# Rotary embedding: whole batches with 32 KB rows, and loads and stores in one in-order queue

## The chip, the cores and the metric

One core of one Trainium2 chip. The metric is the device time in microseconds (us), as a median of several executions. Each kernel was also executed once under the profiler. A profile's span is about 1.8 us shorter than the time of the same execution.

## The reference

```python
# x: 8 batches x 2048 positions x 8 heads x 64, float32; cos, sin: 2048 x 32
x1, x2 = x[..., :32], x[..., 32:]
out1 = x1 * cos - x2 * sin
out2 = x1 * sin + x2 * cos
out = concatenate([out1, out2], axis=-1)
```

x and the output are 33.55 MB each, the tables 0.26 MB each. Every byte is read or written once.

## The kernel before

A partition holds 16 consecutive positions, so a batch is 128 rows of 32 KB. The kernel cuts each batch into two slabs of 2 MB with rows of 16 KB. Loads are issued on the sync queue, stores on the scalar queue, and nine slab buffers lie between them.

```python
    SL = 8                      # positions of a slab, of 16 in a partition
    SLAB = SL * HD              # 4096 floats, 16 KB
    UNIT = 4 * HD
    NBUF = 9
...
    nc.scalar.dma_start(out=cos_sb, in_=cos_src)
    for i in range(NBUF):
        load(i)                 # nc.sync.dma_start, slab 0 in four pieces
...
    kinds = {}
    for i in (5, 10):
        kinds |= {(i, 0): "C", (i, UNIT): "B"}
```

A usual piece of 128x2048 (kind A) is two products of 128x1024 on GpSimd and one product and one addition on VectorE. Kind B leaves the addition to TensorE (two products with the identity matrix, summed in PSUM) and the copy out of PSUM to ScalarE. Kind C takes GpSimd out as well: VectorE makes both products, TensorE sums.

```python
        keep(nc.vector.tensor_mul(out=t1..., in0=xk, in1=rep(cos_ps[...], 2 * H)))
        if kind == "A":
            keep(nc.vector.tensor_add(out=xt, in0=t1, in1=t2))
...
    for i in range(last + 1):
        if i == last:
            for k in range(i - LAG, i):
                store(k, 0, SLAB)          # nc.scalar.dma_start
        for lo, n in spans(pieces(i)):
            rotate(i, lo, n)
            if i == last:
                store(i, lo, n)
        if LAG <= i < last:
            store(i - LAG, 0, SLAB)
        if i > LAG and i - LAG - 1 + NBUF <= last:
            load(i - LAG - 1 + NBUF)
```

Of the kernel before, what the change touches and what calls it, by code (L numbers as in the profile page):

```python
# [9 lines left out]
@with_exitstack  # L10
def kernel(
    ctx: ExitStack,
    tc: tile.TileContext,
    x: bass.AP,
    cos: bass.AP,
    sin: bass.AP,
    out: bass.AP,
):
    nc = tc.nc
    keep = tc.keep_in_program_order  # L20
    f32 = mybir.dt.float32
    PSUM = bass.MemoryType.PSUM

    B, S, H, D = x.shape
    Dh = D // 2
    P = 128
    HD = H * D
    R = S // P

    SL = 8  # L30
    n_half = R // SL
    SLAB = SL * HD
    UNIT = 4 * HD
    NBUF = 9
    C = 512

    xv = x.rearrange("b (q r) h d -> b q (r h d)", q=P)
    ov = out.rearrange("b (q r) h d -> b q (r h d)", q=P)
    cos_src = cos.rearrange("(q r) d -> q r d", q=P)
    sin_src = sin.rearrange("(q r) d -> q r d", q=P)  # L40

    const_pool = ctx.enter_context(tc.tile_pool(name="const", bufs=1))
    tab_pool = ctx.enter_context(tc.tile_pool(name="tab", bufs=1, space=PSUM))
    t1_pool = ctx.enter_context(tc.tile_pool(name="t1p", bufs=1, space=PSUM))
    o_pool = ctx.enter_context(tc.tile_pool(name="op", bufs=2, space=PSUM))
    t1s_pool = ctx.enter_context(tc.tile_pool(name="t1s", bufs=3))
    xpool = ctx.enter_context(tc.tile_pool(name="xpool", bufs=NBUF))
    t2_pool = ctx.enter_context(tc.tile_pool(name="t2p", bufs=3))

    cos_sb = const_pool.tile([P, R, Dh], f32, tag="cb")  # L50
    sin_sb = const_pool.tile([P, R, Dh], f32, tag="sb")
    nsin = const_pool.tile([P, R, Dh], f32, tag="ns")
    eye = const_pool.tile([P, P], f32, tag="eye")
    neye = const_pool.tile([P, P], f32, tag="neye")
    cos_ps = tab_pool.tile([P, R, Dh], f32, tag="cp")
    sin_ps = tab_pool.tile([P, R, Dh], f32, tag="sp")

    slabs = [(b, l) for l in range(n_half) for b in range(B)]
    last = len(slabs) - 1
    xts = {}  # L60

    def cuts(i):
        if i == 0:
            return [HD, HD, 2 * HD, UNIT]
        return [SLAB]

    def pieces(i):
        if i == 0:
            return [HD, HD, 2 * HD, UNIT]
        if i == last:  # L70
            return [UNIT, 2 * HD, HD, HD]
        return [UNIT, UNIT]

    def spans(sizes):
        lo = 0
        for n in sizes:
            yield lo, n
            lo += n

    def load(i):  # L80
        b, l = slabs[i]
        xt = xpool.tile([P, SLAB], f32, tag="xt", name=f"xt{i}")
        for lo, n in spans(cuts(i)):
            nc.sync.dma_start(
                out=xt[:, lo : lo + n],
                in_=xv[b, :, l * SLAB + lo : l * SLAB + lo + n],
            )
            if i == 0 and lo == 0:
                nc.sync.dma_start(out=sin_sb, in_=sin_src)
        xts[i] = xt  # L90

    nc.scalar.dma_start(out=cos_sb, in_=cos_src)
    for i in range(NBUF):
        load(i)

    nc.gpsimd.memset(eye, 0.0)  # L96
    nc.gpsimd.affine_select(
        out=eye,
        in_=eye,
        compare_op=mybir.AluOpType.not_equal,  # L100
        fill=1.0,
        base=0,
        pattern=[[-1, P]],
        channel_multiplier=1,
    )
    nc.scalar.mul(nsin, sin_sb, -1.0)  # L106
    nc.scalar.mul(neye, eye, -1.0)
    nc.vector.tensor_copy(cos_ps, cos_sb)  # L108
    nc.scalar.copy(sin_ps, sin_sb)  # L109

    def rep(a, n):
        return dataclasses.replace(a, ap=[a.ap[0][:], a.ap[1][:], [0, n], a.ap[-1][:]])

    kinds = {}
    for i in (5, 10):
        kinds |= {(i, 0): "C", (i, UNIT): "B"}

    def rotate(i, lo, n):
        b, l = slabs[i]
        kind = kinds.get((i, lo), "A")  # L120
        xt = xts[i][:, lo : lo + n]
        r0 = l * SL + lo // HD
        nr = n // HD
        xk = xt.rearrange("p (r k d) -> p r k d", r=nr, d=Dh)
        xu = xt.rearrange("p (g u d) -> p g u d", u=2, d=Dh)
        if kind == "A":
            t1 = t1_pool.tile([P, n], f32, tag="t1")
        else:
            t1 = t1s_pool.tile([P, n], f32, tag="t1s")
        if kind == "C":  # L130
            t2 = t1s_pool.tile([P, n], f32, tag="t1s")
        else:
            t2 = t2_pool.tile([P, n], f32, tag="t2")
        t1u = t1.rearrange("p (g u d) -> p g u d", u=2, d=Dh)
        t2u = t2.rearrange("p (g u d) -> p g u d", u=2, d=Dh)
        if kind != "C":
            for u, tab in ((1, sin_sb), (0, nsin)):
                nc.gpsimd.tensor_mul(  # L138
                    out=t2u[:, :, u, :].rearrange("p (r h) d -> p r h d", h=H),
                    in0=xu[:, :, 1 - u, :].rearrange("p (r h) d -> p r h d", h=H),  # L140
                    in1=rep(tab[:, r0 : r0 + nr, :], H),
                )
        keep(
            nc.vector.tensor_mul(  # L144
                out=t1.rearrange("p (r k d) -> p r k d", r=nr, d=Dh),
                in0=xk,
                in1=rep(cos_ps[:, r0 : r0 + nr, :], 2 * H),
            )
        )
        if kind == "A":  # L150
            keep(nc.vector.tensor_add(out=xt, in0=t1, in1=t2))  # L151
        elif kind == "B":
            for j in range(n // C):
                o = o_pool.tile([P, C], f32, tag="o")
                cs = slice(j * C, (j + 1) * C)
                nc.tensor.matmul(o, eye, t1[:, cs], start=True, stop=False)  # L156
                nc.tensor.matmul(o, eye, t2[:, cs], start=False, stop=True)  # L157
                keep(nc.scalar.copy(xt[:, cs], o))  # L158
        else:
            keep(  # L160
                nc.vector.tensor_mul(  # L161
                    out=t2.rearrange("p (r k d) -> p r k d", r=nr, d=Dh),
                    in0=xk,
                    in1=rep(sin_ps[:, r0 : r0 + nr, :], 2 * H),
                )
            )
            G = C // Dh
            for u in range(2):
                for j in range(n // 2 // C):
                    o = o_pool.tile([P, C], f32, tag="o")  # L170
                    gs = slice(j * G, (j + 1) * G)
                    nc.tensor.matmul(o, eye, t1u[:, gs, u, :], start=True, stop=False)  # L172
                    nc.tensor.matmul(  # L173
                        o, eye if u else neye, t2u[:, gs, 1 - u, :], start=False, stop=True
                    )
                    keep(nc.scalar.copy(xu[:, gs, u, :], o.rearrange("p (g d) -> p g d", d=Dh)))  # L176

    LAG = 2

    def store(i, lo, n):  # L180
        b, l = slabs[i]
        keep(
            nc.scalar.dma_start(
                out=ov[b, :, l * SLAB + lo : l * SLAB + lo + n],
                in_=xts[i][:, lo : lo + n],
            )
        )

    for i in range(last + 1):
        if i == last:  # L190
            for k in range(i - LAG, i):
                store(k, 0, SLAB)
        for lo, n in spans(pieces(i)):
            rotate(i, lo, n)
            if i == last:
                store(i, lo, n)
        if LAG <= i < last:
            store(i - LAG, 0, SLAB)
        if i > LAG and i - LAG - 1 + NBUF <= last:
            load(i - LAG - 1 + NBUF)  # L200


# [28 lines left out]
```

## Time and profile before

| | before |
|---|---|
| time, median of 3 (later 6) runs | 164.75 (164.68) us |
| span of the profiled run | 163.0 us |
| bytes moved | 67.66 MB, mean 415 GB/s |
| share of 16 DMA engines' span in use | 98.2% |
| VectorE, GpSimd busy | 88%, 86% |
| packet of 16 KB on one DMA engine | 611 ns |

Read the DMA share first.

### The profile page before, as it was taken

The page shows a single profiled execution, that of the slowest core. Times are in us where ns is not written, and L with a number is a line of the kernel's source. Part 1 is how long each engine was busy: PE and PEld are TensorE (multiplying, and loading weights), DVE is VectorE, ACT ScalarE, POOL GpSimd, SP SyncE. Part 2 cuts the span into 40 slices and gives each one's busy share as a digit, 9 for nine tenths or more (in the row PEclk, how much of TensorE's full clock was granted, in tenths as well). Part 3 has the DMA queues.
Part 4 walks back from the last instruction along what each step waited for, and adds up shares of the span by engine and source line. Part 5 has one row for each costly group of instructions (what it writes and reads, how often), then busy time and mean ns, then how long its engine had stood idle before and what let it go on. Part 6 is the DMA issues. An engine that isn't in the chain of part 4 may idle for free. (4 is left out here: it accounts for less than half of the span.)

```text
span 163.0 us, 480 instructions
## 1 busy us (share of the span) xinstructions
PE 33.3 (20%) x64; PEld 13.4 (8%) x64; DVE 143.4 (88%) x71; ACT 12.0 (7%) x20; POOL 139.4 (86%) x74
## 2 busy tenths in 40 slices
PE   0000000000000079993000000899920000000000
PEld 0000000000000024440000000244400000000000
DVE  0587999999999999999899999999999999999900
ACT  3300000000000002232000000022410000000000
POOL 1599999999999999799999999956999999995000
PEclk9999999999999999999555555579997555555555
DMA  4999999999999999999999999999999999999995
GB/s 137 383 432 442 406 398 426 438 438 418 438 434 426 430 434 430 426 434 438 422 428 438 424 422 446 430 414 446 434 422 430 442 422 422 446 426 430 434 402 207
DMA packets 5763, 67.66 MB, mean 415 GB/s; under 512 B 640, under 2 KB 640, under 8 KB 1664
## 3 DMA queue, kind: packets, MB, share of 16 engines
q1 hardware_dynamic: 2880, 33.82, 49.5%
q10 hardware_dynamic: 2880, 33.82, 48.7%
q14 instruction: 3, 0.02, 0.0%
HBM read 34.08 MB, written 33.55 MB: 415 GB/s over the span
## 5 line engine op out<-in xcount | busy, mean ns | idle before, releaser
L138 POOL TENSOR_TENSOR t<-xt,sin_sb 128x1024 f32<-128x1024 f32 (+2 forms) x34 | 70.7, 2081 | 10.8 <-DVE xt L151 6.3
L144 DVE TENSOR_TENSOR t<-xt,cos_ps 128x2048 f32<-128x2048 f32 (+2 forms) x36 | 73.9, 2056 | 1.0
L138 POOL TENSOR_TENSOR t<-xt,nsin 128x1024 f32<-128x1024 f32 (+2 forms) x34 | 70.8, 2082 | 0.0
L151 DVE TENSOR_TENSOR xt<-t,t 128x2048 f32<-128x2048 f32 (+2 forms) x32 | 64.8, 2025 | 5.6 <-POOL t L138 2.1
L172 PE MATMUL o<-t,eye 128*128 128x512 f32 x16 | 11.3, 800 | 85.8 <-DVE t L144 85.8
L176 ACT COPY xt<-o 128x512 f32<-128x512 f32 x8 | 4.7, 586 | 94.5 <-DVE t L144 55.3
L172 PEld LDWEIGHTS o<-t,eye 128*128 128x128 f32 x16 | 3.9, 256 | 90.6 <-issue 90.6
L156 PE MATMUL o<-t,eye 128*128 128x512 f32 x16 | 8.2, 592 | 0.0
L157 PE MATMUL o<-t,eye 128*128 128x512 f32 x16 | 8.2, 592 | 0.0
L173 PE MATMUL o<-t,neye 128*128 128x512 f32 x8 | 6.2, 862 | 0.2 <-DVE t L161 0.2
L158 ACT COPY xt<-o 128x512 f32<-128x512 f32 x8 | 4.7, 586 | 9.0 <-PE o L157 9.0
L108 DVE COPY cos_ps<-cos_sb 128x512 f32<-128x512 f32 x1 | 0.7, 694 | 5.0 <-DMA cos_sb<-in_cos_dram 5.0
L161 DVE TENSOR_TENSOR t<-xt,sin_ps 128x2048 f32<-128x2048 f32 x2 | 4.6, 2281 | 0.0
L173 PE MATMUL o<-t,eye 128*128 128x512 f32 x8 | 4.1, 592 | 0.0
L157 PEld LDWEIGHTS o<-t,eye 128*128 128x128 f32 x16 | 3.0, 190 | 3.8 <-issue 3.8
L156 PEld LDWEIGHTS o<-t,eye 128*128 128x128 f32 x16 | 3.0, 190 | 3.8 <-issue 3.8
L173 PEld LDWEIGHTS o<-t,neye 128*128 128x128 f32 x8 | 2.0, 278 | 4.9 <-issue 3.3
L173 PEld LDWEIGHTS o<-t,eye 128*128 128x128 f32 x8 | 1.5, 190 | 1.9 <-issue 1.9
L106 ACT ACT_TABLE_LOAD x1 | 1.3, 1283 | 1.2 <-PEq L215 1.2
L106 ACT ACTIVATE nsin<-sin_sb 128x512 f32<-128x512 f32 x1 | 0.6, 630 | 3.2 <-DMA sin_sb<-in_sin_dram 3.2
L109 ACT COPY sin_ps<-sin_sb 128x512 f32<-128x512 f32 x1 | 0.6, 579 | 0.0
L96 POOL MEMSET eye<- 128x128 f32 x1 | 0.2, 205 | 0.3 <-POOLq L215 0.3
(6 smaller groups left out, 1.0 us busy)
## 6 DMA issues: line engine op xcount, KB each, us to landing
xt<-in_x_dram SPq DMA_DIRECT2D x15, 2048.0 KB, 27.6
out_dram<-xt ACTq DMA_DIRECT2D x15, 2048.0 KB, 15.3
xt<-in_x_dram SPq DMA_DIRECT2D x1, 1024.0 KB, 7.8
out_dram<-xt ACTq DMA_DIRECT2D x1, 1024.0 KB, 10.3
xt<-in_x_dram SPq DMA_DIRECT2D x2, 256.0 KB, 4.3
xt<-in_x_dram SPq DMA_DIRECT2D x1, 512.0 KB, 5.8
out_dram<-xt ACTq DMA_DIRECT2D x1, 512.0 KB, 8.9
out_dram<-xt ACTq DMA_DIRECT2D x2, 256.0 KB, 7.6
```

The costliest lines, as they stand in the source:

```text
L106: nc.scalar.mul(nsin, sin_sb, -1.0)
L108: nc.vector.tensor_copy(cos_ps, cos_sb)
L138: nc.gpsimd.tensor_mul(out=t2u[:, :, u, :].rearrange("p (r h) d -> p r h d", h=H), in0=xu[:, :, 1 - u, :].rearrange("p (r h) d -> p r h d" ...
L144: nc.vector.tensor_mul(out=t1.rearrange("p (r k d) -> p r k d", r=nr, d=Dh), in0=xk, in1=rep(cos_ps[:, r0 : r0 + nr, :], 2 * H),)
L151: keep(nc.vector.tensor_add(out=xt, in0=t1, in1=t2))
L156: nc.tensor.matmul(o, eye, t1[:, cs], start=True, stop=False)
L157: nc.tensor.matmul(o, eye, t2[:, cs], start=False, stop=True)
L158: keep(nc.scalar.copy(xt[:, cs], o))
L161: nc.vector.tensor_mul(out=t2.rearrange("p (r k d) -> p r k d", r=nr, d=Dh), in0=xk, in1=rep(sin_ps[:, r0 : r0 + nr, :], 2 * H),)
L172: nc.tensor.matmul(o, eye, t1u[:, gs, u, :], start=True, stop=False)
L173: nc.tensor.matmul(o, eye if u else neye, t2u[:, gs, 1 - u, :], start=False, stop=True)
L176: keep(nc.scalar.copy(xu[:, gs, u, :], o.rearrange("p (g d) -> p g d", d=Dh)))
```

## The change

The intent: longer rows make fewer and longer packets, and one queue with a fixed order makes the sequence of loads and stores certain. Five batches of 4 MB are loaded ahead; then each store is followed by the reload of the buffer that the store before it freed. TensorE gets one piece in each of five batches (two of kind C, three of kind B), where it had two of each. Not in the cut below: the kernel before went through the first halves of all batches and then the second halves, the pool of one kind of temporary (t1s) shrinks from three tiles to two, and more of the arithmetic is held to the program's order.

```diff
-    NBUF = 9
+    ROW = R * HD
+    NBUF = 5
...
-    def load(i):                       # slab of 16 KB rows, sync queue
+    def load(b):
+        xt = xpool.tile([P, ROW], f32, tag="xt", name=f"xt{b}")
+        for lo, n in spans([UNIT, UNIT, 2 * UNIT] if b == 0 else [ROW]):
+            keep(nc.sync.dma_start(out=xt[:, lo : lo + n], in_=xv[b, :, lo : lo + n]))
+            if b == 0 and lo == 0:
+                keep(nc.sync.dma_start(out=cos_sb, in_=cos_src))
+                keep(nc.sync.dma_start(out=sin_sb, in_=sin_src))
+        xts[b] = xt
...
-            nc.scalar.dma_start(       # store
+    def store(b, lo, n):
+        keep(nc.sync.dma_start(out=ov[b, :, lo : lo + n], in_=xts[b][:, lo : lo + n]))
...
-    for i in (5, 10):
-        kinds |= {(i, 0): "C", (i, UNIT): "B"}
+    for b, kind in ((1, "C"), (2, "B"), (3, "C"), (4, "B"), (5, "B")):
+        kinds[(b, 0)] = kind
...
+    for b in range(B):
+        done = 0
+        outs = list(spans([2 * UNIT, UNIT, UNIT] if b == last else [ROW]))
+        for lo, n in spans(pieces(b)):
+            rotate(b, lo, n)
+            done = lo + n
+            while outs and sum(outs[0]) <= done:
+                store(b, *outs.pop(0))
+        if b >= 1 and b - 1 + NBUF <= last:
+            load(b - 1 + NBUF)
```

So the queue holds, in this order: load 0 to 4, store 0, store 1, load 5, store 2, load 6, store 3, load 7, store 4 to 7.

More of the change, by code (lines that the diff above doesn't have):

```diff
@@ L28 @@
     R = S // P
-    SL = 8
-    n_half = R // SL
-    SLAB = SL * HD
+    ROW = R * HD
     UNIT = 4 * HD
-    NBUF = 9
+    NBUF = 5
     C = 512
+    last = B - 1
     xv = x.rearrange("b (q r) h d -> b q (r h d)", q=P)
@@ L45 @@
     o_pool = ctx.enter_context(tc.tile_pool(name="op", bufs=2, space=PSUM))
-    t1s_pool = ctx.enter_context(tc.tile_pool(name="t1s", bufs=3))
+    t1s_pool = ctx.enter_context(tc.tile_pool(name="t1s", bufs=2))
     xpool = ctx.enter_context(tc.tile_pool(name="xpool", bufs=NBUF))
@@ L56 @@
     sin_ps = tab_pool.tile([P, R, Dh], f32, tag="sp")
-    slabs = [(b, l) for l in range(n_half) for b in range(B)]
-    last = len(slabs) - 1
     xts = {}
-    def cuts(i):
-        if i == 0:
-            return [HD, HD, 2 * HD, UNIT]
-        return [SLAB]
-    def pieces(i):
-        if i == 0:
-            return [HD, HD, 2 * HD, UNIT]
-        if i == last:
-            return [UNIT, 2 * HD, HD, HD]
-        return [UNIT, UNIT]
     def spans(sizes):
@@ L78, in spans @@
             lo += n
-    def load(i):
-        b, l = slabs[i]
-        xt = xpool.tile([P, SLAB], f32, tag="xt", name=f"xt{i}")
-        for lo, n in spans(cuts(i)):
-            nc.sync.dma_start(
-                out=xt[:, lo : lo + n],
-                in_=xv[b, :, l * SLAB + lo : l * SLAB + lo + n],
-            )
-            if i == 0 and lo == 0:
-                nc.sync.dma_start(out=sin_sb, in_=sin_src)
-        xts[i] = xt
-    nc.scalar.dma_start(out=cos_sb, in_=cos_src)
-    for i in range(NBUF):
-        load(i)
+    def load(b):
[8 more added lines that the diff above has]
+        keep(nc.sync.dma_start(out=ov[b, :, lo : lo + n], in_=xts[b][:, lo : lo + n]))
+    for b in range(NBUF):
+        load(b)
     nc.gpsimd.memset(eye, 0.0)
@@ L105 @@
     )
-    nc.scalar.mul(nsin, sin_sb, -1.0)
-    nc.scalar.mul(neye, eye, -1.0)
-    nc.vector.tensor_copy(cos_ps, cos_sb)
-    nc.scalar.copy(sin_ps, sin_sb)
+    keep(nc.scalar.mul(nsin, sin_sb, -1.0))
+    keep(nc.scalar.copy(sin_ps, sin_sb))
+    keep(nc.scalar.mul(neye, eye, -1.0))
+    keep(nc.vector.tensor_copy(cos_ps, cos_sb))
     def rep(a, n):
@@ L114, with rotate @@
     kinds = {}
-    for i in (5, 10):
-        kinds |= {(i, 0): "C", (i, UNIT): "B"}
-    def rotate(i, lo, n):
-        b, l = slabs[i]
-        kind = kinds.get((i, lo), "A")
-        xt = xts[i][:, lo : lo + n]
-        r0 = l * SL + lo // HD
+    for b, kind in ((1, "C"), (2, "B"), (3, "C"), (4, "B"), (5, "B")):
+        kinds[(b, 0)] = kind
+    def rotate(b, lo, n):
+        kind = kinds.get((b, lo), "A")
+        xt = xts[b][:, lo : lo + n]
+        r0 = lo // HD
         nr = n // HD
@@ L137, in rotate @@
             for u, tab in ((1, sin_sb), (0, nsin)):
-                nc.gpsimd.tensor_mul(
-                    out=t2u[:, :, u, :].rearrange("p (r h) d -> p r h d", h=H),
-                    in0=xu[:, :, 1 - u, :].rearrange("p (r h) d -> p r h d", h=H),
-                    in1=rep(tab[:, r0 : r0 + nr, :], H),
+                keep(
+                    nc.gpsimd.tensor_mul(
+                        out=t2u[:, :, u, :].rearrange("p (r h) d -> p r h d", h=H),
+                        in0=xu[:, :, 1 - u, :].rearrange("p (r h) d -> p r h d", h=H),
+                        in1=rep(tab[:, r0 : r0 + nr, :], H),
+                    )
                 )
@@ L175, in rotate, with pieces @@
                     )
-                    keep(nc.scalar.copy(xu[:, gs, u, :], o.rearrange("p (g d) -> p g d", d=Dh)))
-    LAG = 2
-    def store(i, lo, n):
-        b, l = slabs[i]
-        keep(
-            nc.scalar.dma_start(
-                out=ov[b, :, l * SLAB + lo : l * SLAB + lo + n],
-                in_=xts[i][:, lo : lo + n],
-            )
-        )
-    for i in range(last + 1):
-        if i == last:
-            for k in range(i - LAG, i):
-                store(k, 0, SLAB)
-        for lo, n in spans(pieces(i)):
-            rotate(i, lo, n)
-            if i == last:
-                store(i, lo, n)
-        if LAG <= i < last:
-            store(i - LAG, 0, SLAB)
-        if i > LAG and i - LAG - 1 + NBUF <= last:
-            load(i - LAG - 1 + NBUF)
+                    keep(
+                        nc.scalar.copy(
+                            xu[:, gs, u, :], o.rearrange("p (g d) -> p g d", d=Dh)
+                        )
+                    )
+    def pieces(b):
+        if b == 0:
+            return [2 * HD, 2 * HD, UNIT, UNIT, UNIT]
+        if b == last:
+            return [UNIT, UNIT, UNIT, 2 * HD, 2 * HD]
+        return [UNIT] * 4
+    for b in range(B):
[8 more added lines that the diff above has]
+            load(b - 1 + NBUF)
 _INS = ['x', 'cos', 'sin']
```

## The prediction

> **What bounds the kernel now.** I read the page first: the busy shares, the row of DMA slices and the shares of the DMA queues.
>
> ```profile
> span 163.0 us, 480 instructions
> ...
> PE 33.3 (20%) x64; PEld 13.4 (8%) x64; DVE 143.4 (88%) x71; ACT 12.0 (7%) x20; POOL 139.4 (86%) x74
> ...
> DMA  4999999999999999999999999999999999999995
> GB/s 137 383 432 442 406 398 426 438 438 418 438 434 426 430 434 430 426 434 438 422 428 438 424 422 446 430 414 446 434 422 430 442 422 422 446 426 430 434 402 207
> DMA packets 5763, 67.66 MB, mean 415 GB/s; under 512 B 640, under 2 KB 640, under 8 KB 1664
> ...
> q1 hardware_dynamic: 2880, 33.82, 49.5%
> q10 hardware_dynamic: 2880, 33.82, 48.7%
> ```
>
> The reader is to see that the DMA engines are full from the second slice to the last but one, and that the loads (q1) and the stores (q10) together take 98.2% of 16 engines' span, while VectorE and GpSimd are at 88% and 86%. So the bytes bound the kernel, and the arithmetic is close behind. The chain of waits names DVE and a store, which at first looks otherwise; it only follows the last instructions back. The windows view decides it: the rate and the DMA share of each stretch.
>
> ```profile
> 30.00:50.00 20.00, 0.00 (x0) 0.00 (x0) 19.45 (x9) 0.00 (x0) 20.00 (x10) 1.00 1.00 430
> 130.00:150.00 20.00, 0.00 (x0) 0.00 (x0) 19.33 (x10) 0.00 (x0) 18.12 (x12) 0.50 1.01 433
> ```
>
> The last two columns are the DMA share and GB/s: 1.00 and 430 in the middle, the same 100 us later, whatever the engines do. At 430 GB/s the 67.66 MB need 157.3 us of the 163.0.
>
> Then the trace's packet records (one row for each packet that a DMA engine moved: start, size, duration), because the change alters packet sizes. The medians are 84 ns for 2 KB, 159 ns for 4 KB, 309 ns for 8 KB and 611 ns for 16 KB, for loads and for stores alike. Doubling from 8 to 16 KB costs 302 ns, so a packet is about 7 ns plus 302 ns for each 8 KB. From 16 engines, 16 KB in 611 ns is 429 GB/s, which is the plateau of the page. Stores alone, after 150 us, have the same 611 ns, and loads alone do too once the first few us are over. Nothing in the mixture of directions limits the rate: each DMA engine works at its own fixed pace.
>
> One engine's 163.0 us can be accounted for: about 1.9 us before the first packet; 240 packets of 16 KB (146.6 us), 16 of 8 KB (4.9), 16 of 4 KB (2.5) and 48 of 2 KB (4.0), in sum 158.1; 40 completion packets of 9 ns (0.4); about 0.9 us after the last packet. That makes 161.3. The other 1.7 us is net loss: slow and idle patches while the first small loads, two tables and the first store start, and engines that end unevenly in the last 2 us.
>
> **What the Trainium skill says.** "DMA: Bandwidth & Descriptors", section "Where 436 GB/s comes from", gives a ceiling of 435.2 GB/s for the 16 ports. The trace agrees: 302 ns for 8 KB is 434 GB/s without the fixed part of a packet, and 429 with it at 16 KB. So no arrangement of the same bytes can gain much over 1%. The same page, "Why small descriptors are slow (HBM only)", says that each packet has a small fixed overhead of a few cycles; the 7 ns above is what this trace shows of it. "Issuing engines are not separate DMA queues" says that transfers of several issuers interleave on the same 16 engines and that a second issuer saves only issue time. The trace agrees in that two queues together do not pass 433 GB/s in a steady stretch. "Queues, rings and completion order" says that each DMA engine consumes one row's descriptors in ring order. This matters for the single queue: a transfer stalls only if nothing is queued ahead of it. No run here shows that yet.
>
> **The change, part by part.**
>
> Packets. 14 of the 16 whole-batch transfers get rows of 32 KB, so an engine has 112 packets of 32 KB. An estimate from the fit is 4 x 302 + 7 = 1215 ns each, 136.1 us. The first load and last store are cut in pieces: 16 packets of 16 KB (9.8 us), 32 of 8 KB (9.9); the tables are 16 of 2 KB (1.3). In sum 157.1 us against 158.1, and 22 completion packets instead of 40 (0.2 against 0.4). This saves 1.2 us, all of it on the path. If a 32 KB row is still sent as two packets of 16 KB, the sum is 157.9, and 0.4 us is saved.
>
> Head and tail. The first piece is 1 MB in 8 KB rows instead of 256 KB in 2 KB rows, and only one queue starts; the last store is 1 MB instead of two of 256 KB. I choose to take 0.4 us off the 1.7 us of net loss for it. The first 1.9 us and the last 0.9 us stay.
>
> One queue, in order. A store in it blocks the loads behind it until its batch is computed. I laid the queue out at 9.75 us for each 4 MB (4.194 MB at 430 GB/s), starting effectively at 3 us, which is where the before kernel's 2.93 MB in the first 10 us put it. The five loads and tables end at about 53 us; then store 0 to 63, store 1 to 72, load 5 to 82, store 2 to 92, load 6 to 102, store 3 to 111, load 7 to 121, and stores 4, 5, 6 to 150, store 7 to 160.
>
> Against it stands the compute. VectorE needs 4.73 us for a usual quarter batch (in the chain, a multiply starts at 111.51 and the next at 116.24), GpSimd 4.55 (in the timeline its sine products start at 20.02 and 24.57). VectorE has 27 usual quarters with two operations, two kind-C quarters with two, three kind-B quarters with one: 61 operations of 2.365 us, 144.3 us. GpSimd has 30 quarters, 136.7 us. The tables now follow 1 MB in the queue, so I expect the start at about 7.5 us instead of 5.7, and VectorE's end at about 153 us. Batches are then done at about 28, 47, 63, 82, 99, 117, 135 and 153 us; the queue wants them at 53, 63, 82, 102, 121, 131, 141, and for the last 1 MB piece 158. The least slack is some 5 us, for the last piece.
>
> The other condition: load 5 reuses store 0's buffer and can be issued at about 64 us, when store 1 still has 8 us to run. Load 6 waits for store 1 (72) with load 5 and store 2 queued, load 7 for store 2 (92) with load 6 and store 3 queued. So I expect no bubble.
>
> Compute moves. One kind B more takes one addition of 2.29 us off VectorE, and adds four copies of 0.59 us and matmuls to ScalarE and TensorE, which are at 7% and 20%. All of this is beside the DMA and worth nothing by itself; it buys the slack above.
>
> Sum: 1.9 + 157.1 + 0.2 + 0.9 + 1.3 = 161.4 us of span. The time of 164.75 us is 1.75 us over the span of 163.0, so I add that: 163.15, say 163.2 us, 0.9% below.
>
> **The rivals.** First, **the queue runs dry**: store 0 waits too long, or load 5 to 7 come late because they wait for a store's completion. For it speaks that before 9 buffers of 2 MB decoupled two queues, and now one waiting issue blocks everything behind it. Against it speaks the slack of 5 to 25 us. If each of the three reloads left a hole of 2 us, it would make 169 us.
>
> Second, **VectorE and GpSimd become the bound**. They start about 2 us later, and only 5 us of slack is left at the end. If GpSimd or VectorE ran 4% slower beside the new traffic, the last store would come late by 1 to 2 us: some 164 to 165. In the before kernel the 2.29 and 2.33 us stay equal from 20 us to 140 us under full DMA load, so I give it little.
>
> Third, **32 KB rows bring nothing**: they are split, or one in-order queue overlaps less between packets than two queues do (the windows show a DMA share of up to 1.14 in the first us, where two queues overlap). That makes 164.0 to 165.
>
> Fourth, **a larger gain**: the net loss of 1.7 us goes altogether. This gives 161.8, still short of 2%.
>
> **Range and chances.** The centre is 163.2. Fourth rival at the lower edge, second and third at the upper: 161.8 to 165.0 for 8 in 10. Faster by over 2% means below 161.5, under the best sum that I can form; I give 0.06. Slower by over 2% needs 168 and holes in the queue; 0.05. Within 2%: 0.89.
>
> **What would show it right or wrong.** Packets of 32 KB with a median near 1215 ns would confirm the first step; 16 KB at 611 ns would refute it. The slices should stand at 9 throughout, with 430 to 433 GB/s; a slice at 5 to 8 near 62, 73 or 92 us would be the dry queue, and then the sync queue's own waits should show loads that wait for stores while no packets move. VectorE's last addition should end near 153 us, and the last 1 MB store should be issued some 5 us ahead of the end of the piece before it; if DMA is idle before it, the compute was the bound. The prediction would be wrong if 32 KB packets, or stores and loads in long phases of one direction, ran at another pace than the 611 ns per 16 KB that both have now.

## More of the kernel before

The end deserves a view of its own, one row for each us, with the DMA share and GB/s last:

```profile
158.00:159.00 1.00, 0.00 (x0) 0.00 (x0) 0.00 (x0) 0.00 (x0) 0.00 (x0) 0.50 0.95 393
159.00:160.00 1.00, 0.00 (x0) 0.00 (x0) 0.00 (x0) 0.00 (x0) 0.00 (x0) 0.50 1.02 408
160.00:161.00 1.00, 0.00 (x0) 0.00 (x0) 0.00 (x0) 0.00 (x0) 0.00 (x0) 0.50 0.93 356
161.00:162.00 1.00, 0.00 (x0) 0.00 (x0) 0.00 (x0) 0.00 (x0) 0.00 (x0) 0.50 0.17 64
```

The engines are full nearly to 161 us and then stop almost together.

## The result

165.19 us median (164.66 to 165.66, 6 runs) against 164.68 us (164.61 to 164.78, 6 runs): ratio 1.0028, 95% interval 1.0007 to 1.0049. The two differ by less than 2%, and so do all runs below from the kernel before, except e14 and e15; what is said of such small differences rests on the intervals and on the traces. Ratios here are the mean time of one kernel's fast runs over that of the other's fast runs of the same rounds, so they are not quite the ratio of the medians. Executions over 1.5% slower than the fastest of the same kernel are left out of the means. The kernel is 0.3% slower, where 0.9% faster was forecast, and its runs scatter six times as widely. The page after:

```profile
span 163.0 us, 460 instructions
...
PE 48.0 (29%) x80; PEld 18.9 (12%) x80; DVE 140.1 (86%) x66; ACT 14.3 (9%) x24; POOL 138.9 (85%) x70
...
DMA  5999899899899999999999999999999999999992
DMA packets 3170, 67.65 MB, mean 415 GB/s; under 512 B 352, under 2 KB 352, under 8 KB 608
...
q1 hardware_dynamic: 3168, 67.63, 97.5%
```

The packets fell from 5763 to 3170, and their time from 98.2% to 97.5% of 16 engines' span. That is the gain that was sought; yet the span is the same. The windows show where it went, first at the change from load 4 to store 0, then at the end:

```profile
49.00:51.00 2.00, 2.00 (x3) 0.97 (x4) 2.00 (x1) 0.00 (x0) 2.00 (x2) 0.50 0.61 262
51.00:53.00 2.00, 2.00 (x3) 0.80 (x3) 1.90 (x2) 0.26 (x1) 2.00 (x1) 0.50 1.23 377
...
158.00:159.00 1.00, 0.00 (x0) 0.00 (x0) 0.00 (x0) 0.00 (x0) 0.00 (x0) 0.50 1.04 442
159.00:160.00 1.00, 0.00 (x0) 0.00 (x0) 0.00 (x0) 0.00 (x0) 0.00 (x0) 0.50 0.74 311
160.00:161.00 1.00, 0.00 (x0) 0.00 (x0) 0.00 (x0) 0.00 (x0) 0.00 (x0) 0.50 0.18 74
161.00:162.00 1.00, 0.00 (x0) 0.00 (x0) 0.00 (x0) 0.00 (x0) 0.00 (x0) 0.50 0.06 25
```

A share of short windows is rough, because a packet of 1.2 us is booked where it starts (0.61 and then 1.23 at 49 to 53 us). Over the two windows the rate is 320 GB/s. At the end most engines are done before 160 us, which is over 1 us earlier than before. One or two work on past 161 us: a share of 0.06 is one engine of 16.

The dry queue is not the cause. The sync queue's own waits (total us, times, longest) and VectorE's last addition, in order of time:

```profile
SPq L74 <- DVE xt L135: 96.4, 9, 18.5
SPq L67 <- DMA out_dram<-xt: 36.5, 3, 16.6
```

```profile
151.08 1.23 DVE L135 TENSOR_TENSOR xt<-t,t 128x1024 f32<-128x1024 f32 x1
```

The issuing sequencer waits often, but the reloads were issued at 63.7, 73.5 and 93.2 us, with one or two transfers still queued ahead of each. The last store was issued at 152.3 us and its engines reached it at 157.3 at the earliest.

**The view that decides.** In the trace every transfer leaves one 4-byte completion packet on each of the 16 DMA engines. For each transfer I sorted its 16 completion times. The table (worked out from the packet records) gives the median engine and how far the last engine is behind it. Times worked out from packet records, here, below and in the prediction, stand on a clock that reads 0.23 us more than that of the profile views (which put the end of the last packet at 161.7 us); differences are not touched by it.

```
changed kernel                      median us   last engine behind the median, us
load 3                                42.89        0.18
load 4   (then a store)               53.37        0.51
store 0                               63.05        0.51
store 1                               72.74        0.50
load 5   (then a store)               82.54        0.72
store 2                               92.22        0.72
load 6   (then a store)              101.99        1.22
store 3                              111.68        1.21
load 7   (then a store)              121.38        1.73
store 4                              131.06        1.73
last piece of store 7                160.19        1.73
```

A 4 MB transfer takes 9.7 to 9.8 us on the median engine, except load 4, which takes 10.48: all engines lose about 0.8 us ahead of the first store. After that, the distance of the last engine grows only in loads that are followed by a store. It does not grow in a store, nor in loads 1 to 3, which have a load behind them. The trace does not name the engine of a packet, but the records can be chained by matching each end to the next start. Then the packets that lengthen are mostly the last one or two 32 KB packets of the load (up to 2.2 us at the first change and up to 1.8 us at the later ones, in place of 1.213).

The chains also show a second cost. The engine that ended last stood at the median up to store 2 and fell 1.24 us back in load 6. Of this 0.93 us is an instruction fetch on that engine at 94.6 us (0.31 us for itself, 0.62 us on the packet behind it); the rest, and 0.52 us in load 7, lie at the changes. The next engine carried no fetch and was 1.36 us behind at the end, 1.2 us of it from the four changes. So without the fetch the end would have come some 0.4 us earlier (an estimate: 1.73 - 1.36). The end of the kernel is the end of the last engine, at 161.9 us, while the median engine ended at 160.2, against about 161.4 before.

### The profile page after: what moved, and what is told of

Same layout as the page of the kernel before. It is cut to its first block, busy times and chain, and to the rows that moved or that the text cites. A ratio compares the mean times of both kernels' runs of the same rounds, so it can differ in the third digit from the quotient of the medians.

```text
span 163.0 us, 460 instructions
## 1 busy us (share of the span) xinstructions
PE 48.0 (29%) x80; PEld 18.9 (12%) x80; DVE 140.1 (86%) x66; ACT 14.3 (9%) x24; POOL 138.9 (85%) x70
## 2 busy tenths in 40 slices
DMA packets 3170, 67.65 MB, mean 415 GB/s; under 512 B 352, under 2 KB 352, under 8 KB 608
## 3 DMA queue, kind: packets, MB, share of 16 engines
q1 hardware_dynamic: 3168, 67.63, 97.5%
## 4 chain that ended last, share of the span: by engine, by line
DVE 66%; POOL 17%; issue 6%; DMA 3%; SPq 0%; DVEq 0%; POOLq 0%
DVE t L128 34%; DVE xt L135 30%; POOL t L121 17%; DMA sin_sb<-in_sin_dram 3%; DVE t L145 3%; DVEq L135 0%; SPq L69 0%; SPq L67 0%; POOLq L121 0%
## 5 line engine op out<-in xcount | busy, mean ns | idle before, releaser
L121 POOL TENSOR_TENSOR t<-xt,sin_sb 128x1024 f32<-128x1024 f32 (+1 forms) x32 | 70.8, 2213 | 8.6 <-DMA sin_sb<-in_sin_dram 5.6
L128 DVE TENSOR_TENSOR t<-xt,cos_ps 128x2048 f32<-128x2048 f32 (+1 forms) x34 | 73.4, 2166 | 0.8
L121 POOL TENSOR_TENSOR t<-xt,nsin 128x1024 f32<-128x1024 f32 (+1 forms) x32 | 70.8, 2213 | 0.0
L135 DVE TENSOR_TENSOR xt<-t,t 128x2048 f32<-128x2048 f32 (+1 forms) x29 | 62.2, 2145 | 5.3 <-POOL t L121 2.4
L140 PE MATMUL o<-t,eye 128*128 128x512 f32 x24 | 18.0, 843 | 25.2 <-DVE t L128 25.2
L156 PE MATMUL o<-t,eye 128*128 128x512 f32 x16 | 10.2, 726 | 36.7 <-DVE t L128 36.7
L141 PE MATMUL o<-t,eye 128*128 128x512 f32 x24 | 15.8, 746 | 0.0
L142 ACT COPY xt<-o 128x512 f32<-128x512 f32 x12 | 7.0, 585 | 48.1 <-PE o L141 48.1
L140 PEld LDWEIGHTS o<-t,eye 128*128 128x128 f32 x24 | 5.8, 258 | 34.0 <-issue 34.0
L161 ACT COPY xt<-o 128x512 f32<-128x512 f32 x8 | 4.7, 586 | 42.7 <-PE o L157 42.7
L156 PEld LDWEIGHTS o<-t,eye 128*128 128x128 f32 x16 | 3.5, 236 | 41.1 <-POOL t L121 30.5
L141 PEld LDWEIGHTS o<-t,eye 128*128 128x128 f32 x24 | 6.2, 260 | 9.1 <-issue 9.1
L157 PE MATMUL o<-t,neye 128*128 128x512 f32 x8 | 5.7, 801 | 0.2
L157 PE MATMUL o<-t,eye 128*128 128x512 f32 x8 | 4.1, 592 | 0.0
L157 PEld LDWEIGHTS o<-t,eye 128*128 128x128 f32 x8 | 1.5, 190 | 1.9 <-issue 1.9
```

Of the source, the lines that this page charges most:

```text
L121: nc.gpsimd.tensor_mul(out=t2u[:, :, u, :].rearrange("p (r h) d -> p r h d", h=H), in0=xu[:, :, 1 - u, :].rearrange("p (r h) d -> p r h d" ...
L128: nc.vector.tensor_mul(out=t1.rearrange("p (r k d) -> p r k d", r=nr, d=Dh), in0=xk, in1=rep(cos_ps[:, r0 : r0 + nr, :], 2 * H),)
L140: nc.tensor.matmul(o, eye, t1[:, cs], start=True, stop=False)
L141: nc.tensor.matmul(o, eye, t2[:, cs], start=False, stop=True)
L142: keep(nc.scalar.copy(xt[:, cs], o))
L156: nc.tensor.matmul(o, eye, t1u[:, gs, u, :], start=True, stop=False)
```

## The experiments

Theory A: in one in-order queue each change from load to store costs time on the DMA engines, unequally, and the slowest engine sets the end. Its rivals: the 32 KB rows (B), the later start of the arithmetic (C), and two refinements that came up on the way, of which the main one is A': an instruction fetch in the middle of the run throws one engine out of step, and the changes make that worse. (The other is the pair A1 and A2, explained at e6.) The runs were made in four groups, each against runs of the kernel before on the same chip (medians 164.50, 164.77, 164.78 and 164.78 us).

| run | queues, rows | changes load to store | median us (range) | ratio to before |
|---|---|---|---|---|
| changed kernel | 1, 32 KB | 4 | 165.19 (164.66 to 165.66) | 1.0028 |
| e4 the same again | 1, 32 KB | 4 | 165.08 (164.35 to 165.64) | 1.0023 |
| e1 | 2, 32 KB | - | 164.30 (164.08 to 164.48) | 0.9979 |
| e2 | 1, 16 KB | 4 | 164.32 (164.03 to 164.76) | 0.9983 |
| e3 | 1, 16 KB | 7 | 165.96 (165.65 to 166.43) | 1.0084 |
| e5 | 2, 16 KB | - | 164.71 (164.51 to 164.83) | 0.9993 |
| e6 short last load | 1, 30 + 2 KB | 4 | 165.02 (164.28 to 165.46) | 1.0009 |
| e7 early store | 1, 32 KB | 4 | 165.27 (164.95 to 165.48) | 1.0020 |
| e8 early store | 2, 32 KB | - | 163.96 (163.82 to 164.19) | 0.9951 |
| e9 copy only | 1, 32 KB | 4 | 164.32 (163.90 to 165.32) | 0.9980 |
| e10 copy only | 2, 32 KB | - | 163.04 (162.93 to 163.62) | 0.9902 |
| e11 three tiles | 1, 32 KB | 4 | 164.86 (164.67 to 165.26) | 1.0006 |
| e12 three tiles, early store | 2, 32 KB | - | 164.83 (164.78 to 164.91) | 1.0002 |
| e13 two changes | 1, 32 KB | 2 | 163.83 (163.69 to 164.52) | 0.9953 |

### e1: stores on their own queue

```diff
-        keep(nc.sync.dma_start(out=ov[b, :, lo : lo + n], in_=xts[b][:, lo : lo + n]))
+        keep(nc.scalar.dma_start(out=ov[b, :, lo : lo + n], in_=xts[b][:, lo : lo + n]))
```

> The changed kernel with one edit: its stores are issued on the scalar queue, so loads and stores are again two queues; rows stay 32 KB. Theory A (in one in-order queue each DMA engine stands still at a change from load to store, by 0.1 to 1 us, unequally, and the slowest of 16 engines sets the end): the lengthened 32 KB packets at 51, 81, 101 and 120 us and the uneven ends go; the packet sum stays near 157.0 us per engine; about 163.2 us, ratio to before 0.990 to 0.993. Theory B (32 KB rows or 4 MB transfers as such cost it, for instance by coarse ends): no gain, 165 us, ratio 1.002, engines end as unevenly as in the changed kernel. Theory C (the later start of the arithmetic or the head of one 1 MB load costs it): also 165 us.

Ratio 0.9979 (0.9964 to 0.9994): better than the changed kernel by about 0.8 us, but not the 163.2 us that the prediction and theory A gave. The ends are as even as before; this is the windows view of its end:

```profile
158.00:159.00 1.00, 0.00 (x0) 0.00 (x0) 0.00 (x0) 0.00 (x0) 0.00 (x0) 0.50 1.06 451
159.00:160.00 1.00, 0.00 (x0) 0.00 (x0) 0.00 (x0) 0.00 (x0) 0.00 (x0) 0.50 0.91 385
160.00:161.00 1.00, 0.00 (x0) 0.00 (x0) 0.00 (x0) 0.00 (x0) 0.00 (x0) 0.50 0.06 25
```

The median engine ended at 160.35 us and the last 0.77 us behind. The long packets at 51, 81, 101 and 120 us are gone. What stays is a loss around the first store, at 29 to 35 us: the load packets ahead of it took longer, 1.15 us for each engine in sum. So one queue costs something, and 32 KB rows alone do not make the ends uneven.

### e2, e3 and e5: 16 KB rows, and more changes

e2 cuts each load and store into two transfers of 2 MB, in the same order. e3 also interleaves the halves of a reload with halves of stores. e5 is e2 with the stores on the scalar queue.

```diff
-        for lo, n in spans([UNIT, UNIT, 2 * UNIT] if b == 0 else [ROW]):
+        for lo, n in spans([UNIT, UNIT, 2 * UNIT] if b == 0 else [2 * UNIT] * 2):
...
-        outs = list(spans([2 * UNIT, UNIT, UNIT] if b == last else [ROW]))
+        outs = list(spans([2 * UNIT, UNIT, UNIT] if b == last else [2 * UNIT] * 2))
```

```diff
 # e3 in addition
                 store(b, *outs.pop(0))
+                if ins:
+                    load_part(b - 1 + NBUF, *ins.pop(0))
```

> The changed kernel with each whole-batch load and store cut in two transfers of 2 MB with 16 KB rows, in the same order in the same single queue. Theory A: the changes from load to store are the same four, so the same loss; packets cost 0.8 us more (two of 611 ns for one of 1213 ns: 224 x 611 = 136.9 against 112 x 1213 = 135.9, so 1.0 us): 165.5 to 166.5 us. Theory B (32 KB packets cost it): better than the changed kernel, 163.5 to 164.5 us.

> As the kernel with 16 KB rows in one queue, but each half of a reload follows the first half of a store, so the queue changes from load to store seven times and not four. Theory A: more lost at the changes than with four, by 0.1 to 0.7 us for each added change on the slowest engine: 166 to 168 us, with lengthened packets at each change. Theory B or C: the same as with 16 KB rows in one queue, within 0.3 us. If the queue ran dry because a reload waits for a store, the DMA slices would show a hole of whole us on all engines.

> Fourth cell of the square of queues and row sizes: stores on the scalar queue and every whole-batch transfer as two of 2 MB with 16 KB rows. If queue and row size each cost something by themselves (theory A with the loss at a change growing with the packet in flight), then packets cost 1.0 us more than with 32 KB rows and two queues, the loss around the first store falls from 1.15 to about 0.5 us per engine, and the time is 164.0 to 164.8 us, ratio 0.997 to 1.001, so that with two queues the row size hardly matters. If 32 KB rows are bad as such: under 163.8.

e3 against e2 is as theory A says: three more changes cost 1.64 us (165.96 - 164.32; the intervals are 1.0065 to 1.0103 and 0.9965 to 1.0000), with the same packets. The same table for e3, one row for each load that a store follows:

```
e3, one queue, seven changes        median us   last engine behind the median, us
second half of load 4                 53.50        0.51
first half of load 5                  72.96        0.64
second half of load 5                 82.69        0.85
first half of load 6                  92.41        1.63
second half of load 6                102.18        2.24
first half of load 7                 111.91        2.52
second half of load 7                121.67        2.69
last piece of store 7                160.67        2.63
```

The distance grows at every change after the first (it was 0.56 us ahead of that one), and in the stores between them it stays within 0.01 us. The median engine ended as it did in e2 (160.67 and 160.63 us), so the queue did not run dry; what differs is the last engine, 2.63 us behind in place of 1.12. Chained, the engine that gathers this distance up to load 7 carries no instruction fetch. This is the plainest view of theory A.

e2 is a miss for theory A as I had put it: I expected 165.5 to 166.5 us, and 16 KB rows in one queue were better than 32 KB rows by 0.8 us, although their packets take 1.0 us more. One part of it is seen: at the first change the median engine lost 0.5 us with 16 KB packets (5.39 us for half of load 4 against 4.88), where it lost 0.8 with 32 KB packets. The rest is not shown: e2's profiled run was its slowest (164.76 us), those of the changed kernel and e4 were near their fastest, so their traces hide the difference of the medians. In two queues the order is the other way (e5 0.9993, e1 0.9979), but the intervals overlap (0.9981 to 1.0005, 0.9964 to 0.9994), and the difference of the ratios, some 0.2 us, is less than the 1.0 us of the packets. So that longer rows pay with two queues is not shown; in the one queue they lost more than they gained. e5 also missed on a detail: the loss around the first store was to fall to 0.5 us with 16 KB packets, and chained it was 1.1 us for each engine, as in e1.

### e4: the changed kernel again

> The changed kernel itself, unedited, beside the others on the same chip. 164.7 to 165.7 us as before. Theory A: lengthened packets once more at the four changes from load to store (about 51, 81, 101, 120 us), engines ending over a stretch of 1.5 to 3 us, the last one being the one that lost most at the changes. If the last engine's loss lies elsewhere this time (other packets, other times), the theory falls.

The time and its scatter repeat. The last engine was 1.19 us behind at the end; the distance again grew only in loads ahead of a store (0.59, 0.56, 0.78, 1.19 at the four changes), and load 4 cost the median engine 1.1 us. Most of the last step, 0.46 us, is one packet early in load 7. Here the engine that ended last carried no instruction fetch. Which engine is last and by how much differs between the two traces. That fits the scatter of the times, 1.3 us with one queue against 0.4 us in e1; it is not shown to be its cause.

### e6, e7 and e8: what makes the first change cost 0.8 us?

```diff
 # e6: a short load ahead of each store
-[ROW]
+[ROW - HD, HD]
 # e7 and (two queues) e8: 64 KB stored early, overwritten by store 0 later
+    keep(nc.scalar.dma_start(out=ov[0, :, 0:P], in_=eye))
     keep(nc.scalar.mul(nsin, sin_sb, -1.0))
```

> The changed kernel, one queue, with each 4 MB load cut in one of 30 KB rows and one of 2 KB rows, so that the packet in flight ahead of a store is short. The trace of the changed kernel shows the lengthening on the last load packet ahead of a store. Theory A1 (the loss at a change grows with that packet's length): the loss at 51 us falls from 0.75 to 1.0 us per engine to under 0.3, the later ones nearly vanish; packets cost 0.4 us more; about 164.3 to 164.7 us. Theory A2 (the first store of the run costs about 0.5 to 1 us whatever is in flight): 0.5 to 1.0 us per engine are still lost at 51 us, spread over the 2 KB packets, and the time is 165.3 to 165.8.

> The changed kernel, one queue, with one store of 64 KB (the identity tile, to a place of the output that the first store overwrites later; the result stays right) issued on the scalar queue at about 1.5 us. Theory A2 (the first store of a run is costly, whatever it is): the lengthened packets at 51 us vanish or fall under 0.3 us, some loss appears at 2 to 4 us; the later changes stay; 164.3 to 164.8 us. Theory A1: 0.75 to 1.0 us are still lost at 51 us, 165.1 to 165.5 us.

> The same early 64 KB store with 32 KB rows and two queues. Theory A2: the 1.15 us lost per engine at 29 to 31 us go, 163.2 to 163.6 us, ratio 0.991 to 0.994, the fastest of all. Theory A1: as without it, 164.2 to 164.5.

In e6 the loss at 51 us moved to the last 30 KB packet, which starts over 1 us ahead of the first store, and was 0.5 us for each engine, with 0.1 us more on the 2 KB packets. So it is not tied to the packet just ahead of the store, and A1 falls in this form. In e7 0.64 us were still lost at 51 us, and in e8 0.85 of 1.15 us at 29 to 35 us. A small store beforehand does not take the cost away, so A2 falls as well. The times of e6 and e8 lie between the ranges of the two theories, that of e7 in the range of A1. e8 was nevertheless among the fastest (0.9951, 0.9939 to 0.9963), and why it beats e1 is not shown. Why the first large store costs 0.5 to 1.2 us on every engine, in the kernel before too, stays open.

### e9 and e10: the copy alone

The arithmetic and its set-up are taken out and x is copied, with all transfers and waits for buffers as they were. e10 has its stores on the scalar queue, by the edit of e1. Their outputs are wrong, which doesn't matter for the times.

```diff
-            rotate(b, lo, n)
```

> Wrong on purpose: the changed kernel without any arithmetic, so x is copied to the output through the same one in-order queue, with the same transfers, order and waits for buffers. Theory A' (an instruction fetch in the middle of the run, at 83 to 119 us in every trace so far, takes one DMA engine out of step by about 0.6 us; in one queue an engine out of step loses again at each later change from load to store, and it ends last): with so few instructions there is no fetch in the middle, the loss at 51 us stays (0.6 to 1.0 us per engine), the later ones are small on all engines, and the engines end within 0.8 us of their mean; 163.7 to 164.3 us. Theory A (the changes alone make them uneven): last engine 1 to 2.3 us after the mean as in the changed kernel, 164.5 to 165.6. Theory C (arithmetic or its lateness matters): clearly under 163.5.

> Wrong on purpose: the same copy with the stores on the scalar queue. Theory A': as one queue, or better by the smaller loss at changes only; ends within 0.8 us; 163.4 to 164.2 us. Theory A: 0.8 us or more faster than the copy in one queue.

Two queues copy in 163.04 us and one in 164.32: 1.3 us for the single queue and the order that it imposes, with no arithmetic on the chip. So theory C falls as the cause of that difference: a copy in one queue, which waits for no compute engine, is no faster than the full kernel in two queues. But the arithmetic is not free. Without it the time was shorter by some 0.4 to 0.5% in one queue (0.9980 against 1.0028 and 1.0023) and by 0.8% in two (0.9902 against 0.9979). In e10 the last engine ended 0.3 us behind the median at 160.0; in e9 0.56 behind a median of 160.67. Here all engines lost together, 0.5 us at the last change (load 7 ends 10.2 us after store 3, where 9.7 is usual). No instruction fetch fell into either copy, and e9 came out almost as A' had it (at most 0.8 us behind, 163.7 to 164.3 us). In e4, too, the last engine carried no fetch, yet it ended 1.19 us behind. So fetches are not all that the arithmetic adds; what else makes the same four changes more uneven stays open.

### e11 and e12: three TensorE tiles

```diff
-    for b, kind in ((1, "C"), (2, "B"), (3, "C"), (4, "B"), (5, "B")):
+    for b, kind in ((2, "B"), (4, "B"), (5, "B")):
```

> The changed kernel, one queue, with three TensorE tiles and not five (the two of kind C become usual pieces), so 96 TensorE and weight-load instructions in place of 160. VectorE's work stays the same, GpSimd's grows by 9.1 us to 146, still ahead of the stores' need. Theory A': if TensorE's instructions are the ones fetched at 94.6 us, that fetch goes, the ends draw together to under 1 us behind the mean, 164.2 to 164.6 us. If the fetch stays, the last engine is 1 to 2.3 us late and the time 165.0 to 165.5.

> The best parts together: 32 KB rows, stores on the scalar queue, the early 64 KB store, three TensorE tiles. Theory A': in two queues an engine out of step loses no more, so the fetch matters by 0.3 to 0.6 us at most: 163.4 to 164.0 us, ratio 0.991 to 0.995. If VectorE or GpSimd came to be late for the last stores, over 164.5.

e11 fell between its two ranges; e12 missed the range of A' and fell into the other branch, "over 164.5". Both show the second rival of the prediction at work. GpSimd grows to 147.6 us and VectorE waits for it; its last addition starts at 157.0 us, where it started at 151.1 with five tiles. e11's end:

```profile
157.03 1.23 DVE L135 TENSOR_TENSOR xt<-t,t 128x1024 f32<-128x1024 f32 x1
```

```profile
157.00:158.00 1.00, 0.00 (x0) 0.00 (x0) 0.97 (x1) 0.00 (x0) 0.00 (x0) 0.50 0.38 156
158.00:159.00 1.00, 0.00 (x0) 0.00 (x0) 0.26 (x1) 0.00 (x0) 0.00 (x0) 0.50 0.10 41
159.00:160.00 1.00, 0.00 (x0) 0.00 (x0) 0.00 (x0) 0.00 (x0) 0.00 (x0) 0.50 0.94 393
```

The DMA engines stand idle for over 1 us ahead of the last store: a share of 0.38 and 0.10 with full engines on both sides. In two queues this showed in the time: e12 took 0.9 us more than e8, which has five tiles. In one queue it did not (164.86 us against 165.19 and 165.08). There the last engine was 2.03 us behind the median up to the last store and only 0.25 us behind after it: the others waited for the arithmetic while it caught up. So the tiles are worth having where the engines end evenly. Two instruction fetches were still there (at 96.8 and 98.3 us), so 64 instructions fewer on TensorE and its weight loads did not remove them, and these two runs say nothing on A'.

### e13: two changes in place of four

```diff
-        if b >= 1 and b - 1 + NBUF <= last:
-            load(b - 1 + NBUF)
+        if b == 2:
+            for k in range(NBUF, B):
+                load(k)
```

> The changed kernel, one queue, 32 KB rows, five TensorE tiles, with another order: store 0, 1, 2, then load 5, 6, 7, then store 3 to 7, so the queue changes from load to store twice and not four times. By my layout nothing runs dry (load 5 waits for store 0, done at 63 us; store 2 ends at 82; load 5 lands at 92 and is wanted at 99). If each change costs about 0.3 to 0.5 us on the slowest engine: 164.0 to 164.6 us, ratio 0.996 to 1.000, ends within 1 us of the mean. If only the fetch matters: 164.9 to 165.3, as the changed kernel.

163.83 us, ratio 0.9953 (0.9935 to 0.9971), 1.2 to 1.4 us better than the changed kernel with the same packets in the same single queue, and a little below the 164.0 to 164.6 us that I had expected. The windows at its end, and the table:

```profile
158.00:159.00 1.00, 0.00 (x0) 0.00 (x0) 0.00 (x0) 0.00 (x0) 0.00 (x0) 0.50 1.00 426
159.00:160.00 1.00, 0.00 (x0) 0.00 (x0) 0.00 (x0) 0.00 (x0) 0.00 (x0) 0.50 0.68 287
160.00:161.00 1.00, 0.00 (x0) 0.00 (x0) 0.00 (x0) 0.00 (x0) 0.00 (x0) 0.50 0.06 25
```

```
e13, one queue, two changes         median us   last engine behind the median, us
load 4   (then a store)               53.41        0.32
store 2                               82.49        0.29
load 5   (then a load)                92.17        0.29
load 6   (then a load)               101.88        0.70
load 7   (then a store)              111.60        0.78
last piece of store 7                160.10        0.77
```

The last engine ends at 160.9 us and not at 161.9. The one step of note, 0.4 us in load 6, is not at a change: an instruction fetch took 0.31 us at 95.6 us on that stretch, and chained, it is on the engine that ended last. The one change after it, at load 7, added 0.08 us.

### e14 and e15: many instruction fetches

The copies of e9 and e10 again, with small instructions beside them that touch nothing else:

```diff
+    for _ in range(1500):
+        nc.vector.memset(scratch, 0.0)
```

> Wrong on purpose: the copy in one queue with 1500 memsets of 128x64 on VectorE beside it, which touch nothing else but have to be fetched as instructions along the run. If fetches throw engines out of step and one queue makes this grow: ends 1 to 3 us after the mean, 165 to 167 us, against 164.3 without them. If fetches hardly matter: 164.0 to 164.6.

> The same 1500 memsets beside the copy in two queues. Each fetch packet takes about 0.3 us of one DMA engine; if they fall on different engines: 163.3 to 164.0 against 163.0 without them, and less is added than in one queue. If they all fall on one engine: as much is added in both, 0.3 us for each fetch.

The memsets took 190 ns each and ran to 289 us, so both times are 290.77 us and say nothing; I had expected them to end with the transfers. The traces serve nonetheless. Seven fetches of 8 KB fell between 13 and 161 us, all on one DMA engine. In one queue the last engine's final transfer ended at 166.2 us, in two at 165.9. The median of the others in the one-queue copy was 160.2. Counted packet by packet in that run, a fetch cost its engine 0.7 to 1.0 us: 0.31 us for itself and the rest on the packet behind it. In the one queue the late engine was 2.9 us behind both before and after the change at load 5 (75.9 us against 72.6 to 73.3 for the others at store 1, 85.5 against 82.3 to 83.0 at load 5); at the next two changes it lost 0.2 and 0.0 us. So in this copy an engine out of step did not lose more at a change. That does not settle A' for the full kernel, whose ends are less even than those of the copy without memsets (e9), and whose traces disagree. Chained, the engine with the fetch at about 94 us lost 0.68 and 0.81 us at the next two changes in e7, where the mean engine lost 0.07 and 0.05; it lost 0.39 and 0.54 us in the changed kernel's first profile (mean 0.06 and 0.12), and less than 0.05 us at either in e4. So A' stays open there. What is sure is the plain cost of a fetch in both arrangements: in e1 the distance of the last engine in the stores steps from 0.15 to 0.82 us around the fetch at 97.3 us.

## Why the prediction was wrong

**The packets: right.** 32 KB rows went as single packets of 1213 ns (1215 forecast). The sum is 112 x 1.213 + 16 x 0.611 + 32 x 0.309 + 16 x 0.084 = 156.9 us (157.1 forecast). The extra time at the tail is small (1.07 us after the last packet, not 0.93).

**The order and the slack: right.** No slice near 62, 73 or 92 us shows a dry queue, the reloads went out at 63.7, 73.5 and 93.2 us (64, 72 and 92 forecast), and VectorE ended at 152.3 us (153 forecast). The first and second rivals did not occur, and e11 shows how the second looks when it does.

**The step that failed** is the last term of the sum: "I choose to take 0.4 us off the 1.7 us of net loss for it." I carried over 1.3 us from a kernel with two queues, as if the loss belonged to the start and the end alone. Measured in the profiled run it is 163.0 - (2.0 + 156.9 + 0.2 + 1.1) = 2.8 us. The 0.4 us itself was not far off: chained, the loss of the mean engine in the first 10 us fell from 0.90 to 0.59 us. What the sum had no term for came later. 0.8 us is lost on all engines at the first change from load to store, where the kernel before lost 0.5 us around its first store; 0.3 us on the mean engine at the three later changes; and the last engine is 1.73 us behind the median, where it was 0.7 us behind before. An engine without a fetch was 1.36 us behind, nearly all from the changes; the fetch on the last one moved the end by some 0.4 us more (the estimate above). The profiled run was one of the faster ones, so the median time lies another 0.4 us higher.

**So the expected gain was there and was given back.** The median engine did end 1.2 us earlier than before (160.2 against 161.4), which is what the packets were to save. The end of the slowest engine moved by 0.2 us only (161.9 against 162.1). That the changes within one queue carry the cost is shown three ways: seven against four (+1.64 us), four against two (-1.2 to -1.4 us), and two queues against one (-0.8 us with arithmetic, -1.3 us without). It is no fixed price for each change: e2 has four changes too and lost less than the changed kernel.

**The third rival** had named the place, that "one in-order queue overlaps less between packets than two queues do", with 164.0 to 165. I gave it little weight because I looked for it in the pace of packets, where nothing differs, and not at the changes of direction. What I did give for it was a misreading: I took a DMA share of 1.14 for the overlap of two queues, but the changed kernel, with one, has 1.13 at 6 to 7 us. A share over 1 comes from booking packets where they start. I also read the skill's "Issuing engines are not separate DMA queues" as if one queue and two were equal beyond issue time; e9 and e10 show that here they were not.

What stays open: why a change lengthens the last packets of the load. The skill ("DMA: Bandwidth & Descriptors", section "Two DMAs through the same engine are not ordered") says that an engine's read and write sides are separate queues and that descriptors are pipelined. A load reads memory and writes the buffer, a store the reverse, so at a change both sides may have to turn round, and with a second queue there may be other work for them in that moment. No run here shows the two sides, so this is an argument only. Open too is why 16 KB rows did better than 32 KB rows in one queue by as much as they did.

## What to carry to other kernels

When DMA is full from end to end, follow each of the 16 engines: the slowest one sets the end, and a gain on the average engine is worth nothing until the last one shares it. In one in-order queue, group loads with loads and stores with stores, or put the two on two queues; here either gave 0.5% over the kernel before at best (e13 163.83 us; e8, with its early store, 163.96; two queues alone, e1, gave 0.2%; the bare copy took 163.04). Before thinning out work that looks hidden, check how late the last result may be: three TensorE tiles in place of five used up 5 us of slack, and in two queues this cost 0.9 us.

## What the Trainium skill lacked or had wrong

- "DMA: Bandwidth & Descriptors", "Issuing engines are not separate DMA queues": it says that issuing on several engines only saves issue time. Here the same transfers took 164.32 us in the order of one queue and 163.04 in two (copies), and 165.1 against 164.3 with arithmetic. The cost of a change from load to store within one queue is in no page: from nothing to 0.8 us on the engine that ends last, at each change after the first.
- No page: the first large store of a run costs 0.5 to 1.2 us on every engine, in the packets of the loads ahead of it, in one queue and in two, and an earlier store of 64 KB does not remove it.
- "DMA: Bandwidth & Descriptors", "Queues, rings and completion order", names a runtime-internal row for refills, and "Runtime: NRT & Kernel Launch", "Instruction fetch mechanics", looks at fetches from the engine that runs the instructions; what a fetch costs the DMA engine that carries it is in neither. Here each 8 KB fetch took 0.31 us itself and put its one DMA engine back by 0.4 us (at 108.6 us in the changed kernel) to 1.0 us (in e14); seven of them left one engine some 6 us behind the median of the others.
- "DMA: Bandwidth & Descriptors", "Why small descriptors are slow (HBM only)", works out the fixed part for a packet of 256 bytes only. It is still seen at large ones: 611 ns for 16 KB and 1213 ns for 32 KB, 0.7% apart for each byte.
